# Low-rank gate product of a GLA layer: three parts of 16 inputs stacked in 128 rows, one float32r product a head

## The chip, the cores and the metric

The kernel runs on one core of a Trainium2 chip. The metric is device time in microseconds, the median of several runs. TensorE multiplies, VectorE (DVE) and ScalarE (ACT) do elementwise work, GpSimd (POOL) mostly memsets, and SyncE (SP) issues nearly all transfers from HBM.

## What is computed

The reference is a decoder trunk of two layers with 256 tokens and a width of 1024, all float32. Layer 0 mixes tokens with dilated attention, layer 1 with gated linear attention (GLA); each is followed by a gated convolutional FFN, and every sub-layer is normalised, shifted and scaled by a conditioning vector. The part that matters here is the gate of the GLA: 16 columns of the input projection, glr, go through a low-rank product to 4 heads of 128 gate values each.

```python
def gla_mixer(h, w_in, w_gate, b_gate, g_norm, w_out):
    proj = h @ w_in                     # q, k, v, glr (16 columns), r
    ...
    gk = jax.nn.log_sigmoid((glr @ w_gate + b_gate).astype(jnp.float32)) / B_TAU
    ...
    bcum = jnp.cumsum(gk, axis=3)       # within chunks of 64 tokens
    q_t = q * jnp.exp(bcum)
    k_t = k * jnp.exp(-bcum)
    k_d = k * jnp.exp(blast - bcum)
    ...                                 # chunked attention, state, norm, silu(r), w_out
```

## The kernel before

Activations are kept transposed: 128 rows of features by 256 tokens, 8 such tiles for the width. [...] To keep precision every operand is split into a high part, rounded to float32r, and a low part, what the rounding left. `mm3` (L196) then makes three products: high times high, high times low and low times high.

Weights come in blocks through `split` (L162): one or more DMAs on SyncE into `raw` (4 buffers), a cast on ScalarE (L172) into `whi`, and a subtraction on VectorE (L178) into `wlo` (3 buffers each). Instructions are written in program order, and a planner that simulates the program decides the order on every engine. The author ties the order where it matters: `behind(...)` (L271) makes what is traced inside it queue behind given instructions on the same engine, without waiting for their results. `chain[7]` (L290) holds the last ScalarE and VectorE instruction of a normalisation.

The GLA layer begins when the first FFN's last products end. Its tiles stand in the pool `gla`, in memory that the FFN's tiles had. Slots are given out in the order in which their tags first appear, and a tag has the size of its largest tile. GpSimd fills `keep` (L908), SyncE loads the mask `causal` and the gate weights `w_g` (16 rows by 512, L917), and `all_normed` (L323) makes the normalised input. The loop at L967 computes the values v (`pv`, four banks of 512 columns) from four weight blocks `w_v_b`. After the second block, `log_gates` (L922) is traced: it projects the input on the 16 gate columns (`glr`, 8 x 3 products), copies the 16 rows out of PSUM on VectorE (L929), and `gates_of` (L932) multiplies them by the weights for one head and then for three:

```python
ps = bank("z", "sttt"[hd])
mm(ps[:, :T], w_g[:, P * hd : P * hd + P], glr, start=True, stop=True)   # L940, float32
nc.scalar.activation(nz[:, T * i : T * i + T], ps[:, :T], AF.Identity, scale=-1.0, bias=nbg[:, hd : hd + 1])
```

These four products (`z`) are in plain float32, with 16 rows contracted. What follows on ScalarE and VectorE (absolute value, exponentials, a scan, `e_q`, `e_k`, `e_d`) is needed in `states` (L991), which runs head by head after the values: projections `pqk`, gated `k_d`, `q_t`, `k_t`, a transpose `kdt`, the masked product `a`, the state products `kv`. `output`, `gate` (`pr`), the output projection (`py`) and the second FFN (`pab`, `pd`) come behind. The split of the last value block is tied behind `glr_copy` (L968), the instruction that took glr out of PSUM.

Of the kernel before, what the change touches and what calls it, by code (L numbers as in the profile page):

```python
# [11 lines left out]
F32 = mybir.dt.float32  # L12
EXP_LN = "natural_log_exp_and_others"
F32R = mybir.dt.float32r
U32 = mybir.dt.uint32
AF = mybir.ActivationFunctionType
ALU = mybir.AluOpType

P = 128
D = 1024  # L20
T = 256
# [36 lines left out]
def trunk(ctx: ExitStack, tc: tile.TileContext, I, out):  # L58
    nc = tc.nc
# [12 lines left out]
    def bank(name="ps", tag=None):  # L72
        tag = tag or next(cycle)
        return psum.tile([P, 512], F32, tag=tag, name=name, bufs={"p": 2, "s": 3, "t": 3}[tag])
# [46 lines left out]
    for n in range(2):  # L121
        ps = bank("cb", "t")
# [39 lines left out]
    def split(src, n, dmas=1, after=((), ()), late=(), low=(), lows=True):  # L162
        raw = wraw.tile([P, 2048], F32, tag="raw", name="raw")
        for i in range(dmas):
            c = slice(n * i // dmas, n * (i + 1) // dmas)
            last_load[0] = nc.sync.dma_start(raw[:, c], src[:, c])
        hi = wspl.tile([P, 2048], F32R, tag="whi", name="whi")
        lo = wspl.tile([P, 2048], F32R, tag="wlo", name="wlo")
        for i in range(0, n, n // 2):
            c = slice(i, i + n // 2)  # L170
            with behind(*after[i > 0]):
                copied[0] = nc.scalar.copy(hi[:, c], raw[:, c])  # L172
        if not lows:
            return hi, lo, raw, n // 2
        for i in range(0, n, n // 2):
            c = slice(i, i + n // 2)
            with behind(*(late if i else low)):
                last_lo[0] = nc.vector.tensor_tensor(lo[:, c], raw[:, c], hi[:, c].bitcast(F32), op=ALU.subtract)  # L178
        return hi, lo
# [16 lines left out]
    def mm3(ps, a, b, start, stop):  # L196


        mm(ps, a[0], b[0], start=start, stop=False)  # L199
        mm(ps, a[0], b[1], start=False, stop=False)  # L200
        return mm(ps, a[1], b[0], start=False, stop=stop)  # L201
# [39 lines left out]
    def shift(pool, columns):  # L241

        pad = pool.tile([P, columns], F32, tag=f"pad{len(pads)}", name="pad")
        pads.append(pad)
# [22 lines left out]
    chain = {}  # L267
    squared = [None, None]

    @contextmanager  # L270
    def behind(*those):  # L271

        with ExitStack() as st:
            for i in those:
                st.enter_context(tc.issue_after(i.ins))
            yield
# [76 lines left out]
    def parts(w, at, n=P):  # L353
        return w[0][:, at : at + n], w[1][:, at : at + n]
# [39 lines left out]
    rows_ps, at = [], 0  # L394
    with behind(norm_ops[0]):
        keep_warm(3)
        for i, (g, n) in enumerate(ROWS):
            c = slice(at, at + n)
            ps = bank("rows", "t")[:16, 0:n]
# [209 lines left out]
    for i in range(2):  # L609
        q_pair.append([])  # L610
        for j in range(2):
            at, n = ((112, 2 * T + 112), (0, 2 * T + 16))[j] if i == 0 else (0, 2 * T)
# [283 lines left out]
    def gt(shape, name, dt=F32, bufs=1, tag=None):  # L896
        return gla.tile(shape, dt, tag=tag or name, name=name, bufs=bufs)
# [5 lines left out]
    nc.vector.tensor_scalar(nbg, small[:, C_BG : C_BG + 4], -1.0, None, op0=ALU.mult)  # L903

    PARTS = ((0, 1), (1, NH_B - 1))
    shift(gla, 8)
    keep = gt([P, (NH_B - 1) * T], "keep", tag="D1")
    nc.gpsimd.memset(keep, 1.0)  # L908
# [5 lines left out]

    causal = gt([P, 2, P], "causal")
    nc.sync.dma_start(causal, I["causal"])
    w_g = gt([16, 512], "w_g")  # L917
    nc.sync.dma_start(w_g, I["w_gate"])

    glr_copy = []  # L920

    def log_gates():  # L922
        with behind(*chain[5]):
            w_gl = split(I["w_glr"], 7 * 16 + P)
        ps = bank("glr", "t")
        for kt in range(KT):
            mm3(ps[:, :T], parts(w_gl, 16 * kt), h[kt], kt == 0, kt == KT - 1)
        glr = gt([16, T], "glr")
        glr_copy.append(nc.vector.tensor_copy(glr, ps[:16, :T]))  # L929
        return [gates_of(*part, glr) for part in PARTS]  # L930

    def gates_of(first, n, glr):  # L932
        def new(name, tag, columns=n * T):
            return gt([P, columns], name, tag=f"{tag}{min(first, 1)}")

        nz = new("nz", "A")
        for i in range(n):
            hd = first + i
            ps = bank("z", "sttt"[hd])
            mm(ps[:, :T], w_g[:, P * hd : P * hd + P], glr, start=True, stop=True)  # L940
            nc.scalar.activation(nz[:, T * i : T * i + T], ps[:, :T], AF.Identity,
                                 scale=-1.0, bias=nbg[:, hd : hd + 1])

        ea = new("ea", "B")
        nc.scalar.activation(ea, nz, AF.Abs)
        nc.scalar.activation(ea, ea, AF.Exp, scale=-1.0)
        nc.scalar.activation(ea, ea, AF.Ln, bias=1.0)
        sp = new("sp", "C")
        nc.vector.scalar_tensor_tensor(sp, nz, 0.0, ea, op0=ALU.max, op1=ALU.add)

        cs = new("cs", "cs")
        nc.vector.tensor_tensor_scan(cs, keep[:, : n * T], sp, 0.0, op0=ALU.mult, op1=ALU.add)
        cs3 = cs.rearrange("p (n c) -> p n c", c=CH)
        last = cs3[:, :, CH - 1 : CH]
        dl = new("dl", "C")
        nc.vector.tensor_tensor(dl.rearrange("p (n c) -> p n c", c=CH), cs3,
                                last.to_broadcast([P, 4 * n, CH]), op=ALU.subtract)
        e_d, e_q, e_k = (new(name, t) for name, t in (("e_d", "D"), ("e_q", "A"), ("e_k", "B")))
        nc.scalar.activation(e_d, dl, AF.Exp, scale=1.0 / 16)
        nc.scalar.activation(e_q, cs, AF.Exp, scale=-1.0 / 16)  # L960
        nc.scalar.activation(e_k, cs, AF.Exp, scale=1.0 / 16)
        dec = new("dec", "dec", 4 * n)
        nc.scalar.activation(dec, last.rearrange("p n c -> p (n c)"), AF.Exp, scale=-1.0 / 16)
        return e_q, e_k, e_d, dec

    pv = [[bank("pv", tg) for _ in range(2)] for tg in "ps"]
    for n in range(4):  # L967
        with behind(*((), chain[5], chain[7], glr_copy)[n]):  # L968
            w = split(I["w_v_b"][n], 2048) if n else w_first
            if n > 1:  # L970
                next_ada()
        if n == 0:
            with behind(*chain[7]):
                whole(early_q)
        for i in range(2):
            kt = 2 * n + i
            for t in range(2):
                ht = [y[:, P * t : P * t + P] for y in h[kt]]
                for s in range(2):
                    mm3(pv[t][s], ht, parts(w, D * i + 512 * s, 512), kt == 0, kt == KT - 1)  # L980
        if n == 1:
            gates = log_gates()
# [8 lines left out]
    def states(hd):  # L991
# [14 lines left out]
        e_q, e_k, e_d, dec = gates[part]  # L1006
        own = hd - PARTS[part][0]
        c = slice(T * own, T * own + T)
# [145 lines left out]
    ps = bank("ms")  # L1154
# [119 lines left out]
def build(arrays):  # L1274
    import concourse.bacc as bacc

    nc = bacc.Bacc("TRN2", target_bir_lowering=False, num_devices=1, dynamic_dma_scratch_size=4096)
    I = {
        k: nc.dram_tensor(f"in_{k}", v.shape, mybir.dt.from_np(v.dtype), kind="ExternalInput").ap()
        for k, v in arrays.items()  # L1280
    }
    out = nc.dram_tensor("out_y", (T, D), F32, kind="ExternalOutput").ap()
    with tile.TileContext(nc, schedule_with_timeline_sim=True) as tc:
        trunk(tc, I, out)
    return nc
# [10 lines left out]
```

## Time and profile before

| what | value |
|---|---|
| median of 3 runs | 769.73 us (769.53 to 770.32) |
| span of the profiled execution, first to last instruction | 767.7 us |
| median run minus that span | 2.0 us |
| TensorE, VectorE, ScalarE, GpSimd busy | 759.3, 640.6, 485.5, 13.2 us |
| mean granted TensorE clock | 0.998 |
| GLA layer in the span | from about 464 to 576 us |
| the four z products | 487.0 to 489.0 us |

The page of the profile gives one time for the profiled execution, its span; the runs' times include what lies around it. In a timeline row stand start and length in microseconds, engine, line, operation, output and inputs, shape and count, and in brackets the idle time before with what ended it. Lengths of neighbouring matmuls overlap, since they are pipelined; the step from one start to the next is what a matmul costs in a dense row. A float32 product leaves two records, a float32r product one.

### The profile page before, as it was taken

How to read it: one execution, taken by the hardware profiler on the slowest of the kernel's cores; microseconds unless marked ns; L12 is line 12 of the kernel's file. 1: busy time of each engine (PE TensorE's matmuls, PEld its weight loads, DVE VectorE, ACT ScalarE, POOL GpSimd, SP SyncE). 2: the span in 40 equal slices, each digit the busy share in tenths (PEclk: the TensorE clock that was granted, in tenths of full speed). 3: DMA queues.
4: the chain of work that ended last, by engine and by line, in shares of the span. 5: the costliest groups of instructions: out<-in, count | busy, mean ns of one | idle time of the engine just before them, and what ended most of it. 6: DMA issues, size and time to landing. Idle time of an engine off the chain costs nothing.

```text
span 767.7 us, 15963 instructions
## 1 busy us (share of the span) xinstructions
PE 759.3 (99%) x6430; PEld 739.0 (96%) x6430; DVE 640.6 (83%) x1160; ACT 485.5 (63%) x949; POOL 13.2 (2%) x28
## 2 busy tenths in 40 slices
PE   8999999999999999999999999999999999999997
PEld 6999999999999999999999998899999999999996
DVE  6998988888888869999999778797668899998552
ACT  6477566465646568776767556745767866666552
POOL 1000000000000010000000000000010000000100
PEclk9999999999999999999999999999999999999999
DMA  8989778787787347878646975875355777644531
GB/s 346 402 298 408 269 244 278 255 277 261 278 275 245 112 146 279 333 239 272 235 139 234 353 277 202 328 257 189 131 192 196 251 267 256 239 151 152 192 110 56
DMA packets 35208, 184.72 MB, mean 241 GB/s; under 512 B 6140, under 2 KB 7676, under 8 KB 21182
## 3 DMA queue, kind: packets, MB, share of 16 engines
q1 hardware_dynamic: 34752, 183.26, 67.7%
q8 instruction: 50, 0.82, 0.4%
q10 hardware_dynamic: 382, 0.45, 0.2%
q14 instruction: 24, 0.20, 0.1%
HBM read 182.59 MB, written 1.10 MB: 239 GB/s over the span
## 4 chain that ended last, share of the span: by engine, by line
PE 93%; DMA 3%; ACT 2%; DVE 2%; issue 0%; ACTq 0%
PE pab L200 10%; PE pab L199 10%; PE pab L201 10%; PE pqk L199 5%; PE pqk L201 5%; PE pqk L200 5%; PE pd L200 5%; PE pd L199 5%; PE pd L201 5%; PE pv L200 3%; PE pv L199 3%; PE pv L201 3%; DMA raw<-in_w 2%; PE py L199 2%; PE py L201 2%; PE py L200 2%
## 5 line engine op out<-in xcount | busy, mean ns | idle before, releaser
L172 ACT CAST whi<-raw 128x1024 fp32r<-128x1024 f32 (+4 forms) x270 | 243.7, 946 | 104.0 <-PE pab L200 37.2
L178 DVE TENSOR_TENSOR wlo<-raw,whi 128x1024 fp32r<-128x1024 f32 (+3 forms) x254 | 270.5, 1091 | 44.0 <-ACT whi L172 43.3
L200 PE MATMUL pab<-hlo,whi 128*128 128x256 f32 x672 | 184.6, 276 | 0.0
L201 PE MATMUL pab<-hhi,wlo 128*128 128x256 f32 x672 | 184.6, 276 | 0.0
L199 PE MATMUL pab<-hhi,whi 128*128 128x256 f32 x672 | 183.2, 277 | 0.0
L200 PEld LDWEIGHTS pab<-hlo,whi 128*128 128x128 f32 x672 | 126.0, 188 | 0.2
L201 PEld LDWEIGHTS pab<-hhi,wlo 128*128 128x128 f32 x672 | 126.1, 188 | 0.0
L199 PEld LDWEIGHTS pab<-hhi,whi 128*128 128x128 f32 x672 | 125.1, 188 | 0.1
L140 DVE CUSTOM_DVE_ANT_0 ada_raw<-ada_raw,c_bc 128x1024 f32<-128x1024 f32 x96 | 113.0, 1218 | 5.7 <-DMA ada_raw<-in_w_ada 4.2
L199 PE MATMUL pqk<-hhi,whi 128*128 128x256 f32 x356 | 98.0, 281 | 0.0
L200 PE MATMUL pqk<-hlo,whi 128*128 128x256 f32 x356 | 97.4, 279 | 0.0
L201 PE MATMUL pd<-ghi,wlo 128*128 128x256 f32 x352 | 96.9, 276 | 0.0
L200 PE MATMUL pd<-glo,whi 128*128 128x256 f32 x352 | 96.9, 276 | 0.0
L199 PE MATMUL pd<-ghi,whi 128*128 128x256 f32 x352 | 96.8, 276 | 0.0
L201 PE MATMUL pqk<-hhi,wlo 128*128 128x256 f32 x356 | 96.7, 279 | 0.0
L199 PEld LDWEIGHTS pqk<-hhi,whi 128*128 128x128 f32 x356 | 66.5, 188 | 0.2
L200 PEld LDWEIGHTS pqk<-hlo,whi 128*128 128x128 f32 x356 | 66.7, 188 | 0.0
L201 PEld LDWEIGHTS pqk<-hhi,wlo 128*128 128x128 f32 x356 | 65.9, 188 | 0.7 <-issue 0.7
L200 PEld LDWEIGHTS pd<-glo,whi 128*128 128x128 f32 x352 | 66.0, 188 | 0.0
L201 PEld LDWEIGHTS pd<-ghi,wlo 128*128 128x128 f32 x352 | 66.0, 188 | 0.0
L199 PEld LDWEIGHTS pd<-ghi,whi 128*128 128x128 f32 x352 | 65.9, 188 | 0.0
L852 ACT ACTIVATE r<-pab,small 128x256 f32<-128x256 f32 x86 | 47.4, 559 | 7.3 <-DVE r L855 6.9
(248 smaller groups left out, 1408.8 us busy)
## 6 DMA issues: line engine op xcount, KB each, us to landing
raw<-in_w_up SPq DMA_DIRECT2D x42, 1024.0 KB, 4.9
ada_raw<-in_w_ada SPq DMA_DIRECT2D x29, 1024.0 KB, 5.9
raw<-in_w_down SPq DMA_DIRECT2D x32, 704.0 KB, 4.1
ada_raw<-in_w_ada SPq DMA_DIRECT2D x38, 512.0 KB, 6.4
raw<-in_wqk SPq DMA_DIRECT2D x18, 1024.0 KB, 5.9
raw<-in_wv SPq DMA_DIRECT2D x14, 768.0 KB, 5.9
raw<-in_w SPq DMA_DIRECT2D x7, 960.0 KB, 6.4
raw<-in_w_out_a SPq DMA_DIRECT2D x4, 1024.0 KB, 6.6
```

The source lines that it names most:

```text
L140: i = nc.vector.tensor_tensor_reduce(w, w, c_bc, op0=ALU.mult, op1=ALU.add, scale=1.0, scalar=0.0, accum_out=dot,)
L172: copied[0] = nc.scalar.copy(hi[:, c], raw[:, c])
L178: last_lo[0] = nc.vector.tensor_tensor(lo[:, c], raw[:, c], hi[:, c].bitcast(F32), op=ALU.subtract)
L199: mm(ps, a[0], b[0], start=start, stop=False)
L200: mm(ps, a[0], b[1], start=False, stop=False)
L201: return mm(ps, a[1], b[0], start=False, stop=stop)
L852: nc.scalar.activation(r, u[:, :T], AF.Identity, scale=cw[2], bias=col(C_CB + 44 * l + f))
```

## The change

The weights of the gate are loaded three times, into rows 0, 32 and 64 (16 rows each) of a zeroed tile `w_raw` of 128 rows, which uses the slot `C1`. ScalarE copies it to float32r (`w_g`), and VectorE overwrites rows 64 to 79 with the low part. So `w_g` holds high, high and low parts. A tile `glr` of 128 rows is zeroed as well; its rows 0 to 15 get the high part of the 16 inputs (VectorE), rows 32 to 47 the low part (VectorE), rows 64 to 79 the high part again (ScalarE). One product of 128 rows a head then sums high x high, low x high and high x low, where a float32 product of 16 rows stood. `glr_copy` is now the subtraction. The slot `C1` appears earlier in the pool than before, and so does `glr`.

```diff
     PARTS = ((0, 1), (1, NH_B - 1))
+    STACKED = (0, 32, 64)
...
-    w_g = gt([16, 512], "w_g")
-    nc.sync.dma_start(w_g, I["w_gate"])
+    w_g = gt([P, 512], "w_g", F32R)
+    w_raw = gt([P, 512], "w_raw", tag="C1")
+    nc.gpsimd.memset(w_raw, 0.0)
+    for at in STACKED:
+        nc.sync.dma_start(w_raw[at : at + 16, :], I["w_gate"])
+    with behind(*chain[7]):
+        nc.scalar.copy(w_g, w_raw)
+        own = slice(STACKED[2], STACKED[2] + 16)
+        nc.vector.tensor_tensor(w_g[own, :], w_raw[own, :], w_g[own, :].bitcast(F32), op=ALU.subtract)
 
     glr_copy = []
+    glr = gt([P, T], "glr", F32R)
+    nc.gpsimd.memset(glr.bitcast(F32), 0.0)
...
-        glr = gt([16, T], "glr")
-        glr_copy.append(nc.vector.tensor_copy(glr, ps[:16, :T]))
+        own = [slice(at, at + 16) for at in STACKED]
+        nc.vector.tensor_copy(glr[own[0], :], ps[:16, :T])
+        nc.scalar.copy(glr[own[2], :], ps[:16, :T])
+        glr_copy.append(nc.vector.tensor_tensor(glr[own[1], :], ps[:16, :T], glr[own[0], :].bitcast(F32), op=ALU.subtract))
```

## The prediction, on record before the result

> **What bounds the kernel now.** I began with the page's head: busy times, then the chain that ended last.
>
> ```profile
> span 767.7 us, 15963 instructions
> PE 759.3 (99%) x6430; PEld 739.0 (96%) x6430; DVE 640.6 (83%) x1160; ACT 485.5 (63%) x949; POOL 13.2 (2%) x28
> PE 93%; DMA 3%; ACT 2%; DVE 2%; issue 0%; ACTq 0%
> ```
>
> TensorE is busy for 99% of the span, and 93% of the chain that ended last is its own work. An average can hide a stage with another limit, so I next asked for busy times of the GLA stage, around the edit, in windows (the columns are PE, PEld, DVE, ACT and POOL busy with their instruction counts, then the granted clock, the DMA share and GB/s).
>
> ```profile
> 464.00:490.00 26.00, 26.00 (x127) 21.48 (x126) 21.68 (x39) 17.31 (x39) 1.18 (x4) 1.00 0.78 289
> 490.00:535.00 45.00, 45.00 (x340) 41.40 (x339) 39.42 (x65) 27.66 (x53) 0.62 (x2) 1.00 0.63 227
> ```
>
> TensorE is busy for every microsecond of both, at full clock. So a matmul microsecond removed here comes off the end, and work added to VectorE, ScalarE, GpSimd or the queues costs nothing until it makes a matmul late. The third view is the chain of waits around the gate products (start, length, what).
>
> ```profile
> 486.86 0.23 PE pv L199
> 487.09 1.92 PE z L940 x8
> 489.01 0.43 PE pv L200
> ```
>
> The four float32 products z leave eight records, two each, which take 1.92 us. The pv product behind them takes 0.43 where the one before takes 0.23: leaving float32 costs a further 0.20. The removed block is worth 1.92 + 0.20 = 2.12 us.
>
> **TensorE's side of the change.** Four float32r products of 128 rows and 256 moving columns take the block's place. The trace has thousands of that shape, at two paces (in the timeline: start, length, engine, line, what). The lengths overlap, so the price is the step from start to start.
>
> ```profile
> 454.80 0.28 PE L199 MATMUL pd<-ghi,whi 128*128 128x256 f32 x1
> ...
> 463.30 0.28 PE L199 MATMUL pd<-ghi,whi 128*128 128x256 f32 x1
> ```
>
> ```profile
> 495.01 0.28 PE L199 MATMUL pqk<-hhi,whi 128*128 128x256 f32 x1
> ...
> 497.49 0.28 PE L199 MATMUL pqk<-hhi,whi 128*128 128x256 f32 x1
> ```
>
> There are 75 steps between the first pair: 8.50/75 = 0.113 us. There are 21 between the second: 2.48/21 = 0.118. I take the slower pace, which is that of this stage: 4 x 0.118 = 0.47 us. With the other pace it would be 0.45. Does a float32r group between 512-column products pay the 0.20 at its edge too? The glr products do just that, twice, earlier on:
>
> ```profile
> 474.38 0.28 PE L199 MATMUL glr<-hhi,whi 128*128 128x256 f32 x1
> 474.50 0.28 PE L200 MATMUL glr<-hlo,whi 128*128 128x256 f32 x1
> 474.62 0.40 PE L200 MATMUL pv<-wlo,hhi 128*128 128x512 f32 x1
> 474.85 0.40 PE L201 MATMUL pv<-whi,hlo 128*128 128x512 f32 x1
> ```
>
> Steps of 0.12, 0.12 and 0.23: no edge. So the saving on TensorE is 2.12 - 0.47 = 1.65 us. Its near end, if all the edge stays, is 1.92 - 0.47 = 1.45; its far end, at the quick pace, is 1.67.
>
> [...]
>
> **Operands: weights.** The copy of the gate weights to float32r is 128x512 on ScalarE and the low part is 16x512 on VectorE. Nearest rows, grouped by line and shape (count, busy, mean ns):
>
> ```profile
> L178 DVE TENSOR_TENSOR wlo<-raw,whi 128x512 fp32r<-128x512 f32 x2 | 1.3, 674 | 0.0
> ```
>
> ```profile
> L172 ACT CAST whi<-raw 128x512 fp32r<-128x512 f32 x2 | 1.1, 619 | 2.1 <-DMA raw<-in_w_qk_b 2.1
> ```
>
> So 0.62 and 0.67 us, both ordered behind the last normalised tile, near 474 us on ScalarE and 475.5 on VectorE. Queued behind them are the casts and low parts of the next value weights:
>
> ```profile
> 473.94 2.00 ACT L172 CAST whi<-raw 128x1024 fp32r<-128x1024 f32 x2
> ```
>
> ```profile
> 478.14 2.36 DVE L178 TENSOR_TENSOR wlo<-raw,whi 128x1024 fp32r<-128x1024 f32 x2
> 482.07 0.41 DVE L929 COPY glr<-glr 16x256 f32<-16x256 f32 x1 [1.58 <-PE glr L201]
> ```
>
> ```profile
> 481.88 1.09 PE L199 MATMUL pv<-whi,hhi 128*128 128x512 f32 x4
> 482.81 0.39 PE L200 MATMUL pv<-wlo,hhi 128*128 128x512 f32 x1
> ```
>
> ```profile
> 487.02 1.99 PE L940 MATMUL z<-glr,w_g 16*128 16x256 f32 x8
> ```
>
> The casts end at 475.94 and TensorE wants the high part at 481.88: 0.62 later is 5.3 us early. The low parts end at 480.50 and are wanted from 482.81: 0.67 later still leaves 1.6 us, and VectorE's idle 1.58 us before the glr copy takes the rest up. Cost: nothing. Without that cover it would be at most 0.7 us.
>
> **Operands: the 16 inputs.** One VectorE copy (0.41) becomes that copy, a subtraction of the same 16x256 shape (0.41 again) and a ScalarE copy beside them. The first z product starts at 487.02 and has the copy's result at 482.48; the subtraction puts this to 482.89, so 4.1 us are left. ScalarE waits for a transfer at the time and has room for its copy:
>
> ```profile
> 483.58 0.62 ACT L172 CAST whi<-raw 128x512 fp32r<-128x512 f32 x1 [2.08 <-DMA raw<-in_w_qk_b]
> ```
>
>  The low parts of the last value weights are queued behind the subtraction instead of the copy and move by 0.4 us; their products come after z. Cost: nothing here. If the order that the planner writes should bring z right behind the glr products, the chain of copy and subtraction would stand open instead, for 0.8 us and, with the waits between engines, up to 1.0.
>
> **GpSimd and the transfer queue.** Two memsets are new, w_raw (128x512) and glr (128x256), and two more DMAs, all of which wait for the memory of the FFN stage before, as keep does, and the weight DMAs wait for the w_raw memset as well.
>
> ```profile
> L614 POOL MEMSET q<- 128x512 f32 (+2 forms) x4 | 2.1, 552 | 0.0
> L1022 POOL MEMSET a_t<- 128x256 f32 x4 | 1.2, 316 | 60.8 <-PE o L1065 60.8
> ```
>
> ```profile
> 463.86 0.74 POOL L908 MEMSET keep<- 128x768 f32 x1 [28.31 <-PE pd L201]
> 464.54 0.58 POOL L1022 MEMSET a_t<- 128x256 f32 x2
> 465.07 0.11 POOL L909 MEMSET keep<- 128x12 f32 x1
> ```
>
> ```profile
> 464.25 0.42 SPq L918 DMA_DIRECT2D w_g<-in_w_gate  x1
> 465.59 0.34 SPq L166 DMA_DIRECT2D raw<-in_w_v_b  x1
> ```
>
> ```profile
> raw<-in_w_v_b SPq DMA_DIRECT2D x4, 1024.0 KB, 4.9
> ```
>
> The w_raw memset (0.55) is done by 465.1 if it comes right behind keep's first, by 466.1 if last of all and behind that of glr (0.32). Three issues of 0.42 us on SyncE then end by 466.4 to 467.4, and the value weights queued behind them (465.59 now) go out 0.8 to 1.8 us late. They need 4.9 us to land, so by 472.3, before ScalarE casts them at 473.94. Cost: nothing; without that cover the 5.3 us between cast and use would have to go first. Should the planner put the gate-weight DMAs behind the value weights instead, they are issued by 467.2, still 6.8 us before ScalarE's copy.
>
> **Sum.** -1.65 us on TensorE, 0 elsewhere. The profiled span of 767.7 lies 2.0 us under the median run of 769.73; I take that surround as unchanged: 769.73 - 1.65 = 768.08, so 768.1 us, a gain of 0.21%. A measurement here can tell about 0.2%, or 1.54 us, from no change; the forecast lies just past that bound.
>
> **Rivals.** [...]
>
> Second, slower: the quick and the slow pace. Nothing in the rows tells what picks one; the step went from 0.113 in the FFN to 0.118 in the head stage, with the same shapes. An f32r group where a float32 one stood could leave TensorE in the slow pace past this stage. Each product at the slow pace costs 0.0045 us, so the 1.65 us are gone after 367 products. The gate projections (192), the output projection (192) and the first two FFN groups (72) together make 456 x 0.0045 = 2.1 us, hence 770.2; carried through twenty more FFN groups of 48 it costs 4.3 more, 774.5. Against it stand the float32 products of heads 0 to 3 that lie between, and the pace right behind them:
>
> ```profile
> 530.96 0.28 PE L200 MATMUL pr<-hlo,whi 128*128 128x256 f32 x1
> ...
> 532.66 0.28 PE L200 MATMUL pr<-hlo,whi 128*128 128x256 f32 x1
> ```
>
> 15 steps in 1.70 us, 0.113 each: quick, though the head stage before them was slow.
>
> Third, slower by a new wait: VectorE and ScalarE fall behind, because TensorE runs 1.65 us ahead of work that doesn't.
>
> ```profile
> 501.28 0.41 DVE L1010 TENSOR_TENSOR k_d<-pqk,e_d 128x256 f32<-128x256 f32 x1
> ```
>
> ```profile
> 503.50 0.38 PE L1018 MATMUL kdt<-ident,k_d 128*128 128x128 f32 x2
> ```
>
> Head 0's k_d ends at 501.69, 1.8 us before its transpose. If nothing on VectorE moved up, 0.15 us would be left, no stall. But a planner that swaps in one adaLN product of 1.22 us ahead of k_d makes a wait of 1.1 us, and one at each of the four heads up to 4.3 us: 768.1 + 4.3 = 772.4. It decides from the second such swap on (two give 770.2). A small gain is open too: head stages at the quick pace, 168 products x 0.0045 = 0.8 us, 767.3. That the change does not do what it says I rule out: both operands are float32r tiles.
>
> **How the numbers follow.** The plain sum has 0.48, with 767.7 to 768.5 as its own range (the bounds of the edge and the pace, and 0.3 us for the surround); a little over half of that lies past the 0.2% bound, so 0.27 faster and 0.21 same. The quick pace on top has 0.15, all faster. The partly eaten gain has 0.17, all same. The slow pace has 0.10, half same (770.2) and half slower (carried on). The new wait on VectorE has 0.10, counted as slower. Together: faster 0.27 + 0.15 = 0.42, same 0.21 + 0.17 + 0.05 = 0.43, slower 0.05 + 0.10 = 0.15. The range reaches from below the quick pace, 767.1, to 771.2, which takes in the eaten gain, the slow pace up to the FFN and two swaps with something over; the tails to 772.4 and 774.5 are left out.
>
> **What would show it.** Right: four z records with 128 rows, steps near 0.118, the following pv product at 0.23, and the stretch from the last pv before z to the first after it shorter by about 1.65 us, with the stages before 464 and after 570 unchanged in length. Right in its cover: the glr subtraction ends microseconds before the first z, and the value-weight transfer goes out about 1 us later without any wait of TensorE. Wrong: waits of TensorE on VectorE or ScalarE in the window from 464 to 535, another order of z among pv, or steps of 0.118 in the gate, output or FFN products where they are 0.113 now.

## The result: 779.8 us, slower by 1.3%, and the profile after

The changed kernel takes 779.82 us (median of 4 runs, 779.3 to 780.93). The kernel before, beside it on the same chip, takes 769.89 (769.53 to 770.32). The ratio is 1.013, with a 95% interval of 1.0118 to 1.0143. The forecast was 768.1, with a range of 767.1 to 771.2.

The head of the page of the changed kernel has these lines: the span, the busy times, the shares of the chain that ended last.

```profile
span 777.5 us, 15964 instructions
PE 758.8 (98%) x6426; PEld 739.1 (95%) x6426; DVE 643.1 (83%) x1162; ACT 486.1 (63%) x951; POOL 13.7 (2%) x30
PE 89%; DVE 4%; DMA 3%; ACT 2%; issue 1%; SPq 0%; ACTq 0%; DVEq 0%
```

TensorE is not busier than before (758.8 us, before 759.3), yet the span is 9.8 us longer: it is lost in waiting, not in more work. TensorE's share of the chain fell from 93% to 89%, VectorE's rose from 2% to 4%. The same two windows as in the prediction show where:

```profile
464.00:490.00 26.00, 26.00 (x130) 22.03 (x129) 23.59 (x42) 17.34 (x35) 1.92 (x6) 1.00 0.76 272
490.00:535.00 45.00, 35.45 (x262) 32.98 (x260) 31.36 (x53) 21.91 (x49) 0.62 (x2) 0.89 0.58 211
```

The stage with the new operands and the gate product (464 to 490) is still full. In the next one TensorE is busy for 35.45 of 45 us, and the granted clock is 0.89. TensorE's waits name the instruction (us in total, times, longest):

```profile
PE kdt L1030 <- DVE k_d L1022: 10.1, 2, 9.5
PE kv L1052 <- ACT kdT L1031: 0.5, 1, 0.5
```

Neither line stood among the waits of the kernel before. The transpose of head 0 waits 9.55 us for `k_d`, which VectorE writes 9.81 us later than before (511.09, before 501.28). The chain of waits tells what VectorE did meanwhile (start, length, what):

```profile
488.03 0.47 PE z L952 x4
...
494.88 0.94 ACT whi L172
495.85 2.36 DVE wlo L178 x2
...
500.01 1.12 DVE wlo L178
501.13 1.14 DVE ada_raw L140
502.28 0.76 DVE ada_raw L140
...
503.42 1.67 DVE cs L964
505.09 1.11 DVE wlo L178
...
506.88 1.14 DVE ada_raw L140
508.02 1.14 DVE ada_raw L140
509.17 1.14 DVE wlo L178
510.31 0.87 DVE dl L968
511.17 0.35 DVE k_d L1022
...
511.56 0.69 PE kdt L1030 x2
```

The gate product is down to 0.47 us for four records. From 495.85 on VectorE works without a pause, but much of it on other things: low parts of weights for heads to come (`wlo`), four adaLN products of the next conditioning (`ada_raw`, called dots below) and the 768-wide `dl` of the other heads, all in its queue ahead of `k_d`. Nothing that the change adds stands in this stretch of the queue. What changed in it is the order that the planner wrote; the experiments test whether that is the cause.

### The profile page after: what moved, and what is told of

It is laid out like the page before. It is cut to its first block, busy times and chain, and to the rows that moved or that the text cites. A ratio compares the mean times of both kernels' runs of the same rounds, so it can differ in the third digit from the quotient of the medians.

```text
span 777.5 us, 15964 instructions
## 1 busy us (share of the span) xinstructions
PE 758.8 (98%) x6426; PEld 739.1 (95%) x6426; DVE 643.1 (83%) x1162; ACT 486.1 (63%) x951; POOL 13.7 (2%) x30
## 4 chain that ended last, share of the span: by engine, by line
PE 89%; DVE 4%; DMA 3%; ACT 2%; issue 1%; SPq 0%; ACTq 0%; DVEq 0%
PE pab L201 10%; PE pab L200 10%; PE pab L199 10%; PE pd L201 5%; PE pd L199 5%; PE pd L200 5%; PE pqk L199 5%; PE pqk L201 5%; PE pqk L200 5%; PE pv L200 3%; PE pv L199 3%; PE pv L201 3%; PE py L199 2%; PE py L200 2%; PE py L201 2%; DVE ada_raw L140 2%
```

## The experiments

Three theories were put against each other. **Order**: the order of the queues makes the whole loss, and the product saves what was forecast. **Added work**: the longer chain to the stacked operands makes the gates late, whatever the order. **Pace**: float32r products in place of float32 ones leave TensorE slow.

**The changed kernel in the order of before.** At the end of the trunk every instruction of the GLA layer is tied behind its neighbour on its engine, by a list with the order that the kernel before had; the new instructions are put in where they fit. The computation is the same.

```diff
+    ahead = {i.name: i for i in tc.nc.cur_bb.bb.instructions}
+    for names in ORDER:                       # one list for each engine
+        for first, then in zip(names, names[1:]):
+            tc.add_manual_dep(ahead[then], first, mybir.DependencyInfo(mybir.DependencyClass.NoSync, mybir.DependencyReason.DATA), reason="issue_after")
```

> The changed kernel with every instruction of the gated-attention layer held in the order that the kernel before had on each engine; the new instructions (three weight loads, two memsets, copies and subtractions) are put where they fit, nothing is left out. The order theory: the gates chain of head 0 is no longer queued behind low parts and adaLN dots, k_d of head 0 comes near 501 us again, TensorE does not wait at kdt, and only the product's saving is left: 769.9 - 1.6 = 768.3 us. The added-work theory (the stacked operands themselves make the gates late, whatever the order): kdt still waits some 10 us, 779 us. The pace theory (slow float32r products after the new block): about 770 to 774.

Measured: 769.16 us where before took 769.79, ratio 1.0001 (0.9986 to 1.0017). The loss of 10 us is gone, though all of the added work is there, so the added-work theory fell. But the median is 0.9 us above the 768.3 of the order theory, and the ratio, which one execution of 776.5 us raises, shows no saving. The profile is of that execution, so the same kernel was run again for the stages.

> The changed kernel in the order of before a second time, since its first profile had lost 2.2 us in the first 60 us, where the kernels are the same, and a transfer of w_ada was 4.3 us late in it. The order theory with the slack of before: 768.1 to 769.2 us; k_d of head 0 near 501 us and no wait at kdt over 1 us. Bought back only in part if k_d is late by the 0.4 us that the glr chain took more than predicted, or if a wait for a kdT copy or a later k_d takes it. The added-work theory: 779.

Measured: 769.59 us, before 770.17, ratio 0.9996 (0.9987 to 1.0005), 0.4 us above the range of the order theory. VectorE writes `k_d` of head 0 nearly when it did before (501.28), and TensorE doesn't wait for it:

```profile
501.57 0.42 DVE L1022 TENSOR_TENSOR k_d<-pqk,e_d 128x256 f32<-128x256 f32 x1
```

The profile also shows where most of the missing saving went (timelines of TensorE and ScalarE):

```profile
494.21 0.39 PE L199 MATMUL pqk<-hhi,whi 128*128 128x256 f32 x1 [0.49 <-ACT v L997]
```

```profile
492.53 0.85 ACT L957 ACTIVATE ea<-nz 128x768 f32<-128x768 f32 x1
...
493.57 0.58 ACT L997 COPY v<-pv 128x512 f32<-128x512 f32 x1
```

```profile
521.60 0.48 PE L1052 MATMUL kv<-v,kdT 64*128 64x256 f32 x1 [0.45 <-ACT kdT L1031]
```

TensorE is earlier now, so two things that used to be just in time are late: the first product of head 0 waits 0.49 us for ScalarE to empty a PSUM bank of the value product, a copy that stands behind a 768-wide step of the gates; and later `kv` waits 0.45 us for `kdT`. The first product of head 0 starts at 494.21, 0.80 us before its 495.01 in the kernel before, instead of 1.65.

**The kernel before in the order of the changed one.** The opposite edit: float32 product, no stacked operands, but the queues as the changed kernel has them (the same lines, with that order in the list).

> The kernel before, its float32 gate product and its operands untouched, with each engine's instructions of the layer held in the order that the changed kernel has (the added instructions left out). The order theory: k_d of head 0 comes near 511 us and TensorE waits some 10 us at kdt, so the whole loss and no saving: 769.9 + 9.9 + 1.6 = 781 us, bounds 779.8 to 782. The added-work theory: no added work, so no loss: 770. The pace theory: no new products, 770.

Measured: 781.57 us, before 769.79, ratio 1.0155 (1.0142 to 1.0168). The timeline has the same stall in a kernel that has nothing of the change:

```profile
513.07 0.69 PE L1018 MATMUL kdt<-ident,k_d 128*128 128x128 f32 x2 [9.33 <-DVE k_d L1010]
```

Order alone costs 11.8 us. The changed kernel with the same order lost 9.93, so the change itself is worth 11.78 - 9.93 = 1.85 us there.

**All operands, float32 product.** `w_g` and `glr` are float32 tiles, so the stacked work is all done but the low parts are zero; the planner writes its own order.

```diff
-    w_g = gt([P, 512], "w_g", F32R)
+    w_g = gt([P, 512], "w_g")
...
-    glr = gt([P, T], "glr", F32R)
+    glr = gt([P, T], "glr")
...
```

> The changed kernel with its stacked operands (all copies, subtractions, memsets and loads) but the four gate products in float32 over 128 rows; tiles w_g and glr in float32, so that their low parts come out as zero. No order is pinned: the planner, told of a longer z, writes its own, which has k_d of head 0 ahead of the adaLN dots. The order theory: no wait at kdt; z costs what it did before and the longer chain ahead of it stays within its slack: 769.5 to 770.5 us. The added-work theory: the same operand work, so the same loss and the saving gone: 779 to 782. The pace theory: no float32r block of 128 rows, 770.

Measured: 771.70 us, ratio 1.0031 (1.0021 to 1.0042): 1.2 us more than the order theory's upper end, and far under the 779 of the added-work theory. Head 0 is in time here; the transpose of head 1 is late, with two adaLN products and a low part more ahead of its `k_d` than before:

```profile
512.03 0.44 PE L1030 MATMUL kdt<-ident,k_d 128*128 128x128 f32 x2 [1.02 <-DVE k_d L1022]
```

**High parts alone.** One float32r product of 16 rows, the two products with low parts left out; one load, no memset, one copy of each operand. Nearly nothing is added. The edit is against the kernel before:

```diff
-    w_g = gt([16, 512], "w_g")
-    nc.sync.dma_start(w_g, I["w_gate"])
+    w_g = gt([16, 512], "w_g", F32R)
+    w_raw = gt([16, 512], "w_raw", tag="C1")
+    nc.sync.dma_start(w_raw, I["w_gate"])
+    with behind(*chain[7]):
+        nc.scalar.copy(w_g, w_raw)
...
-        glr = gt([16, T], "glr")
+        glr = gt([16, T], "glr", F32R)
```

> The gate product as one float32r product of 16 rows from high parts alone (the two products with low parts are left out), one weight load, one copy of each operand, no memset; planner's own order, which has k_d of head 0 ahead of the dots. The order theory: 769.9 - 1.65 = 768.2 us. The added-work theory: 768.2 too, since nearly none of the work is added. The pace theory (a float32r block in place of a float32 one slows what follows): 770 to 774.

Measured: 775.44 us, ratio 1.0076 (1.0062 to 1.0089). All three expectations missed: the first two by 7 us, and the pace theory, whose range ends at 774, has no rows for it. Waits of TensorE on VectorE and ScalarE make it slow. The order is a third one, in which the 768-wide `dl` stands behind two adaLN products and two low parts, and `k_d` of head 1 behind `dl`, two more dots and a low part (VectorE's timeline, then TensorE's waits):

```profile
506.28 0.96 DVE L960 TENSOR_TENSOR dl<-cs 128x768 f32<-128x768 f32 x1
...
510.91 0.42 DVE L1014 TENSOR_TENSOR k_d<-pqk,e_d 128x256 f32<-128x256 f32 x1
```

```profile
PE kdt L1022 <- DVE k_d L1014: 2.1, 1, 2.1
PE a L1033 <- DVE k_t L1016: 1.3, 2, 1.1
PE kv L1044 <- ACT kdT L1023: 0.7, 1, 0.7
```

In the kernel before, these two started at 501.94 and 507.37. So a shorter product with one ScalarE copy and its tile added is enough to make the planner write a bad order. Which detail of an edit tips the planner no run here isolates. My expectation had looked at head 0 alone.

**What in the queue costs how much.** In the changed kernel the adaLN products that stood ahead of `k_d` of head 0 are tied behind it; in a second kernel the low parts of two weight blocks as well. All else is left to the planner, so what stands around the moved work can shift as well. The last pair of lines is in the second kernel alone.

```diff
...
-        next_ada()
+        with behind(*first_kd):               # k_d of head 0
+            next_ada()
...
-            w = split(I["w_qk_b"][hd], 2048)
+            w = split(I["w_qk_b"][hd], 2048, **(dict(low=first_kd, late=first_kd) if hd in (2, 3) else {}))
```

> The changed kernel with one order edge: the adaLN dots that the planner put ahead of k_d of head 0 are tied behind it; all else is left to the planner. The order theory: the four dots ahead of k_d took 4 x 1.14 = 4.6 us of VectorE, so k_d of head 0 starts at 506.5 instead of 511.1, the wait at kdt falls from 9.6 to about 5 us: 779.8 - 4.6 = 775.2 us, 774 to 777 with what the dots delay behind k_d. The added-work theory: the dots only fill time in which VectorE waits, so still 779.

> As the run with the dots behind, and the low parts of the weights of heads 2 and 3 tied behind k_d of head 0 as well. The order theory: four more VectorE operations of 1.14 us leave the way, k_d near 502 to 503, no wait at kdt over 1 us: 769 to 770 us, and up to 774 if the low parts, four in a row behind k_d of head 0, now hold up k_d of head 1. The added-work theory: 779.

Measured: 776.11 us for the first (ratio 1.0087, 1.0069 to 1.0104), 773.25 for the second (1.0043, 1.003 to 1.0057), before 770.17. Above before that is 9.9 us with nothing moved, 5.9 with the dots moved, 3.1 with the low parts moved too. The dots were worth 4.0 us (4.6 expected), the low parts 2.9. The second median lies above the 769 to 770 that was expected if nothing else were held up, and inside the wider bound of 774. In the first the wait at head 0 shrinks as it should (the profile is of an execution of 779.43 us), and in the second the remainder lies in other places:

```profile
PE kdt L1033 <- DVE k_d L1023: 5.4, 2, 4.9
```

```profile
PE kv L1055 <- ACT kdT L1034: 1.8, 1, 1.8
PE a L1044 <- DVE k_t L1027: 1.3, 2, 1.1
PE kdt L1033 <- DVE k_d L1023: 1.1, 2, 0.7
```

The low parts now queue behind `k_d` of head 0 and hold up head 1, where `k_d` starts at 510.75 (before 507.37).

**A version that keeps the saving.** From the order of before, ScalarE's copy of the value product is moved ahead of the 768-wide steps; then also, at heads 2 and 3, state updates and `kdT` ahead of an adaLN product that waits for its weights (1.37 us, at 517.61 in the second run with the order of before), and a dot behind `k_d`. As a control the kernel before got the same moves. The edit is in the list of the order (`mod` and `early_x` take up a dot's result):

```diff
 ScalarE:  whi, whi,
-          ea (768), ea (256), v, ea (768), v, ea (768)
+          ea (256), v, ea (768), ea (768), v, ea (768)
 VectorE:  st (head 0),
-          dot, st, dot, st, q_t, k_t, oacc, k_d
+          st, st, dot, q_t, k_t, oacc, k_d, dot
 ScalarE:  mod, early_x (first dot),
-          mod (second dot), osq, kdT, st, ln, rstd, kdT
+          kdT, osq, st, ln, rstd, kdT, mod (second dot)
```

> The changed kernel in the order of before with one move on ScalarE: the first copy of the value product, and the last step of ea of head 0, stand ahead of the two 768-wide steps of ea. In the run with the order of before TensorE stood 0.49 us (0.67 us with its gap) at the first product of head 0 for that copy. The order theory: that wait goes and the keys' products of head 0 start at 493.5 instead of 494.2, but the adaLN dots, which wait for their weights at 517.6, hand back what is not needed at head 3: between no gain and 0.67 us over the run with the order of before, so 768.9 to 769.6 us where before is 770.2. The added-work theory: no change, 769.6.

> As the run with the copy first, and at heads 2 and 3: VectorE updates the states of head 1 ahead of the dot that waits for its weights, and takes the second dot behind k_d of head 3; ScalarE copies kdT of head 2 ahead of the square of o and of the scale from that dot. The order theory: the wait of 0.45 us at kv goes too, the whole saving of 1.65 us of the product reaches the end: 770.2 - 1.65 = 768.5 us, 768.0 to 769.0; below that if the moves free more than the product gave. The added-work theory: 769.6 as with the order of before.

> The kernel before with the same moves on ScalarE and VectorE and its float32 product, everything else in its own order. What the moves give without the change: before had no wait of TensorE at these places, so the order theory expects nothing, 770.2 +- 0.3 us; if it is as fast as the kernel with the moves and the change, the change itself brings nothing.

> The kernel with the moves and the change a second time: 8 of its 12 executions took 768.0 to 768.2 us and 4 took 771.5 to 771.9, so that the interval of the ratio held 1. The order theory: the median stays within 0.4 us of 768.2, 1.6 us under before; executions some 3.4 us longer are those that lose time at the start, where the kernels are the same (other kernels' long executions lost 2 to 4 us in the first 60 us), and come with any of the kernels. If half or more are long, the moves have a cost of their own.

Measured, each within what the order theory expected: 769.09 us with the one move (ratio 0.9994, 0.9985 to 1.0003), 768.17 with all moves and the change, 770.26 with the moves alone (1.0003, 0.9995 to 1.0012), before 769.76. The second run of all moves gave 768.36, before 769.90. The waits at the value copy and at `kv` are gone, and the gate projection `pr`, at 530.75 before, starts 1.38 us earlier (second run of all moves):

```profile
529.37 0.36 PE L199 MATMUL pr<-hhi,whi 128*128 128x256 f32 x1
```

So medians are 1.6 and 1.5 us under before, about the 1.65 of the product, and the control shows that the moves give nothing by themselves. As a ratio, which the longer executions raise, it isn't settled: 0.9993 (0.998 to 1.0005) and 0.9987 (0.9973 to 1.0). Of the 24 executions of the kernel with all moves and the change 17 took 767.6 to 769.1 us and 7 took 771.1 to 771.9. None of those 7 has a profile. Three other profiled executions lie well above the medians of their kernels: the control (773.33), the first run with the order of before (776.5) and the one with the dots tied behind (779.43). All three lose time at the very start, where the kernels are the same: six products (L401) that take 1.47 us together in the kernel before, from 11.22, take 2.74 in the control, from 12.06, and 2.7 with the dots tied behind. From 10 to 20 us TensorE's window has 73 products in the kernel before and 39, 43 and 40 in these three. The granted clock of the control reads 1.00 from 10 to 20 us all the same, so that column does not account for every slow stretch. Why the kernel with all moves was long in 7 of 24 executions, while the kernel before, in the four sessions in which it ran beside the experiments, was over 771 us in 4 of 81, is open.

## Why the prediction was wrong

**What held.** The time on TensorE came out: z takes 0.47 us (0.47 forecast), the value product behind it 0.22, and the first product of head 0 starts 1.64 us earlier (forecast 1.65):

```profile
487.87 0.64 PE L952 MATMUL z<-glr,w_g 128*128 128x256 f32 x4
488.34 0.39 PE L199 MATMUL pv<-whi,hhi 128*128 128x512 f32 x1
...
493.37 0.28 PE L199 MATMUL pqk<-hhi,whi 128*128 128x256 f32 x1
```

**Right as a sum, wrong in a part: the edge.** The prediction put the 0.20 us behind z down to leaving float32. Two of the runs change only the type or only the rows of the product. These are their chains, with float32 and 128 rows, then with float32r and 16 rows:

```profile
488.24 1.73 PE z L952 x8
489.97 0.23 PE pv L200
```

```profile
486.87 0.67 PE z L944 x4
487.54 0.43 PE pv L200
```

| the four z products | z, us | value product behind, us | z and what is over 0.23, us |
|---|---|---|---|
| 16 rows, float32 (before) | 1.92 | 0.43 | 2.12 |
| 128 rows, float32 | 1.73 | 0.23 | 1.73 |
| 16 rows, float32r | 0.67 | 0.43 | 0.87 |
| 128 rows, float32r (changed) | 0.47 | 0.22 | 0.47 |

In these chains the edge goes with the 16 rows, not with float32. Starts in the timelines, from the last value product ahead of z to the second one behind it, less two steps of 0.23, give the same totals to 0.01 us. The type is worth 1.25 us at 16 rows and 1.26 at 128, the full rows 0.39 or 0.40. The sum of 1.65 came out because the change does both, which was luck in this part; float32r with 16 rows saved 1.25, where the expectation for the high parts alone had counted on 1.65. A gain partly eaten at the product, which has 0.17 of the chances, no run with the change shows: TensorE waited for nothing at z, and in the changed kernel the first product of head 0 started 1.64 us earlier. What did eat into the gain, in the order of before, were the two waits further on, 0.49 and 0.45 us.

**Covers.** Those of the operands held, some with less to spare. The copy to float32r took 0.61 us and the low part 0.68; the value weights went out at 466.55, 0.96 us late. The low part, forecast near 475.5 us on VectorE, came at 478.93, behind two adaLN products, and the low parts of the value weights behind it ended at 482.34, 0.5 us before they were wanted (482.83) instead of 1.6. TensorE waited for none of it. z itself stands later among the value products (487.87, before 487.02), another order, which the prediction had named as a sign of being wrong.

The slow pace of the second rival did not come: in `pr` the step is 0.113 us as before (540.92 to 543.98, 27 steps).

**Mis-sized: the chain to glr.** I put ScalarE's copy beside VectorE's work and the chain at 0.8 us. The three writes went one after the other, with 0.04 and 0.03 us from the end of one to the start of the next at the two changes of engine: 482.26 to 483.50, 1.24 us.

```profile
482.26 0.40 DVE L939 CAST glr<-glr 16x256 fp32r<-16x256 f32 x1
```

```profile
482.70 0.36 ACT L940 CAST glr<-glr 16x256 fp32r<-16x256 f32 x1 [0.74 <-DVE glr L939]
```

```profile
483.09 0.41 DVE L941 TENSOR_TENSOR glr<-glr 16x256 fp32r<-16x256 f32 x1 [0.43 <-ACT glr L940]
```

Against z at 487.87 this costs nothing. But all that VectorE has queued behind it comes later. In the second run with the order of before, the dots behind the chain start at 485.89, 1.21 us later than before (484.68), and ScalarE takes the second dot's result ahead of the gates' first step, which starts at 488.60, 0.85 us later (before 487.75):

```profile
488.30 0.39 ACT L148 ACTIVATE mod<-dot,one_b,small 128x1 f32<-128x1 f32 x1 [0.63 <-DVE dot L140]
488.60 0.82 ACT L953 ACTIVATE nz<-z,nbg 128x256 f32<-128x256 f32 x2
```

So it is this delay that met the earlier TensorE at the value copy, and with that copy moved ahead (the run with one move) the wait was gone.

**The step that failed** is the sum's "0 elsewhere". It took the order of the queues as given, although a planner writes it. The third rival named the right place, `k_d` of head 0, and the right cause, adaLN products put ahead of it. Its price was wrong: one swap of 1.22 us ahead of `k_d`, 1.1 us of wait, and 4.3 us for one at each of the four heads. In fact four dots, low parts and a late start came together at head 0. In the kernel before VectorE began the gates (`sp`) at 493.24 and `k_d` at 501.28. In the changed one it began them at 498.13 and 511.09. First before, then changed:

```profile
493.24 0.42 DVE L949 SCALAR_TENSOR_TENSOR sp<-nz,ea 128x256 f32<-128x256 f32 x1
```

```profile
495.85 2.36 DVE L178 TENSOR_TENSOR wlo<-raw,whi 128x1024 fp32r<-128x1024 f32 x2 [1.58 <-ACT whi L172]
498.13 1.29 DVE L961 SCALAR_TENSOR_TENSOR sp<-nz,ea 128x256 f32<-128x256 f32 x2
```

So 4.89 us were lost ahead of the gates, where ScalarE now casts weights first and VectorE waits for it, and 4.92 between the gates and `k_d`: four dots (4 x 1.14 = 4.6 us), a low part (1.1) and the 768-wide `dl` (0.9) came in, and some 1.7 us, mostly the copies of v, left this stretch. I had priced a planner's choice as a swap of neighbours; it was a new schedule.

**Not in the prediction: the cost of the wait itself.** After 9.55 us of idling, TensorE came back at half clock (granted 0.50 from 511.5 to 514.5). From the start of `kdt` to the tenth `pqk` product behind it takes 3.25 us (511.56 to 514.81), in the kernel before 1.72 (503.50 to 505.22):

```profile
505.22 0.28 PE L199 MATMUL pqk<-hhi,whi 128*128 128x256 f32 x1
```

The balance goes by starts. The step from the product ahead of `kdt` to `kdt` is 9.83 us instead of 0.13, so 9.70 more. With -1.64 (z) and +1.53 (the clock) the tenth product is 9.59 us late, and `pr` is 9.97 late (540.72, before 530.75). The 0.38 between hold two further waits, 0.52 at `kdt` of a later head and 0.46 at `kv`; the rest of that stretch is 0.60 us shorter than before, for a reason that was not looked into.

## What to carry to other kernels

Where a planner orders the engines, an edit's price has two parts: its own instructions, which rows of the profile gave closely here (1.65 us forecast on TensorE, 1.64 measured; 0.8 on the chain to glr, 1.24 measured), and a new order, which they don't give and which cost up to 11.8 us here, seven times the saving. Compare the order of the queues around the edit before believing a sum, and hold the old order before judging the edit; tying work behind the one instruction with little slack (1.8 us at `k_d`) left 3.1 us of loss here. And when TensorE moves ahead, list each wait with less slack than the gain: two of them took about 1 us of the 1.65 even in the old order. A block of 16-row products among 128-row ones cost 0.4 us more here than a block of 128 rows, whatever its type.

## What the runs showed that I had not expected

The granted clock fell during the long waits. In the changed kernel TensorE is idle from 502.0 us, and the granted clock (third from the end of a window's row) goes to 0.50. It is full again only at about 514.8, 3.2 us after work began at 511.56 (0.50 from 511.5 to 514.5, 1.00 from 514.8 to 517; from 513.13 to 513.34 is a step of 0.21 us, where it is 0.12 at a clock of 1.00):

```profile
503.00:506.00 3.00, 0.00 (x0) 0.00 (x0) 3.00 (x4) 1.63 (x5) 0.00 (x0) 0.76 0.55 145
506.00:509.00 3.00, 0.00 (x0) 0.00 (x0) 3.00 (x6) 1.61 (x5) 0.00 (x0) 0.50 1.02 374
```

```profile
513.13 0.42 PE L200 MATMUL pqk<-hlo,whi 128*128 128x256 f32 x1
513.34 0.42 PE L201 MATMUL pqk<-hhi,wlo 128*128 128x256 f32 x1
...
514.81 0.28 PE L199 MATMUL pqk<-hhi,whi 128*128 128x256 f32 x1
```

The run with high parts alone had a fall after a wait of only 2.06 us (509.32 to 511.38); this is its window from 511 to 513 us:

```profile
511.00:513.00 2.00, 1.40 (x6) 1.16 (x7) 2.00 (x4) 0.37 (x1) 0.00 (x0) 0.67 0.77 295
```

The return did not take the same time everywhere: in the kernel before with the new order work began again at 513.07, and the clock still reads 0.50 from 515.5 to 517. Nor is the delay of the fall one number: taking each fall as one step from 1.00 to 0.50, the means of the windows put it, as an estimate, 2.6 us after idling began in the changed kernel (0.76 over 503 to 506), 3.3 in the kernel before with the new order (0.67 over 506 to 509, idle from 503.74) and 5.2 with the dots tied behind (0.90 over 509 to 511.5, idle from 505.76), there after work had resumed. Beyond its own length the wait of 9.55 us cost 1.53 us. The wait of 1.02 us with the float32 product left the clock of its stage at 1.00.
